# Encoder layer with expert-choice MoE on one core: norm rows in fp32r parts, gate values in one PSUM tile, last stage summed in PSUM

## The chip, the cores and the metric

The kernel runs on one core of one Trainium2 chip. The metric is the time of one execution on the device in microseconds (us). The kernel before took 981.74 us (median of three executions, 981.29 to 982.71). All times within the profile come from one more execution, which was profiled. TensorE is called PE, VectorE DVE, ScalarE ACT, GpSimd POOL and SyncE SP, as in the profile. L1208 is line 1208 of the kernel before.

## The reference

One layer over 512 tokens of width 1024, all in float32:

```python
z = x @ w_in                      # NA q|k|v, GQA q|k|v, memory q, 3 branch gates
merged = sum_g sigmoid(gate_g) * (branch_g @ w_branch_g)   # three attention mixers
x = LN(alpha * x + merged @ w_out, ln1_g, ln1_b)
aff = softmax(x @ w_router)       # 16 experts
gate, idx = top_k(aff.T, 64)      # each expert chooses 64 of 512 tokens
h = x[idx] @ w_gate_up            # 1024 -> 2 x 1024, per expert
ye = (silu(hg) * hu) @ w_down * gate
x = LN(alpha * x + scatter_add(ye), ln2_g, ln2_b)
```

The weights of the 16 experts are 192 MB, and each is read once.

## The kernel before, in words

**Stages.** The mixers run from 0 to about 452 us, w_out with the first LayerNorm, router and selection to about 523, the 16 experts from 526 to 947, and a tail of 31 us with the last quarter of the last down product, the second LayerNorm and the stores.

**Number form.** Where float32 precision is needed with the faster fp32r products, a tile is split into a high part (ACT rounds to fp32r, `hi_lo`, L85) and a low part (DVE subtracts, L86); products then run as high x high, high x low and low x high. Products with both operands in plain fp32 take PE several passes.

**Mixers.** PE works through units of weights, each split by ACT and DVE ahead of use. Attention units (`GqaUnit` and others) are interleaved with the projections of `run`, which calls small background pieces from the list `bg`; `after[i]` holds what SP is to load after weight unit i.

**Weight ring.** The experts' weights come in 192 loads of 1 MB, all issued by SP, into a ring of 22 slots of SBUF. `ring.done(...)` marks a slot as used once PE is through with it, and only then is the next load for it issued. An expert has 32 gate/up products (`gate_up`, L1208, 64 tokens stationary and 512 weight columns moving; four for each of the eight loads of 128 rows) and 32 of the down product (`down`, L1241).

**Gather.** `gather(qd)` runs before experts 0, 4, 8 and 12. It takes the tokens of four experts through one-hot matrices, and takes the gate values with eight products of 128 x 6 (L1188): two sets of four, each in a PSUM tile of tag Y, which has one buffer (tags mm, S, T and Y have 3, 2, 2 and 1). DVE adds each set up with four reductions (L1193).

**Norm rows.** The four rows ln1_g, ln1_b, ln2_g, ln2_b arrive as 32 pieces of 128 (`lnr`). `ln_row` (L1277) broadcasts a half row to all partitions with four plain fp32 products of a column of the identity with `lnr`. In expert 12 `rows_of_norm` writes the row of ln2_g on all partitions, and builds `gb`, six rows with high and low parts of ln2_g and ln2_b, by eight small products, seven DVE and two ACT operations.

**Last expert and tail** (`last_down`, L1345 on). The output columns are treated in quarters of 256. For each quarter `product(q)` makes the last expert's down product (L1366: 32 products with 64 rows, in two halves of 128 columns that lie on different partitions), `split(q)` splits it (L1375 on ACT, L1377 on DVE), and the combination with the gate matrix g adds it to the accumulator `acc`. For quarters 0 and 1 the combination goes to PSUM, DVE adds it to `acc` (L1390) and takes the statistics (L1392), and POOL multiplies by ln2_g (`times_g`, L1381). For quarters 2 and 3 the accumulator was put into PSUM ahead of time by a plain fp32 identity product in expert 15 (`preload`, L1342), PE adds onto it (L1398), DVE takes statistics out of PSUM (L1402) and multiplies by ln2_g (L1405). The products alternate between banks of tags S and T. Then 22 dummy products (`keep_warm`, L1413) follow on PE, DVE gathers mean and variance (L1434), works out 1/std (y) and −mean·y, and writes them into `ch`, PE transposes `ch` to rows (`rowT`, L1447), ACT copies the rows out (L1449), and the result is y·(acc·g) plus a low-rank product of the rows with `gb` (L1461). Five of the eight tiles of 128 x 512 are finished by DVE (L1473) and stored through SP (L1474); three by PE with a diagonal matrix (L1465) and by ACT (L1478), stored through ACT's queue (L1479).

```python
        product(3)
        add_in_psum(2)
        for m in range(NT):
            stats(2, m)
        split(3)
        add_in_psum(3)
        for mp in range(2):
            times_g_psum(2, mp)
        keep_warm(22)
```

Each engine works through its own instructions in the order in which the code issues them; an instruction waits for the last writer or reader of its tiles.

Of the kernel before, what the change touches and what calls it, by code (L numbers as in the profile page):

```python
# [9 lines left out]
F32 = mybir.dt.float32  # L10
# [4 lines left out]
ALU = mybir.AluOpType  # L15
# [26 lines left out]
def layer_kernel(ctx: ExitStack, tc: tile.TileContext, xt, xn, first0, wu, bgate, rpb, gains, wrt,  # L42
# [200 lines left out]
    lnr = cp.tile([32, P], F32, name="lnr")  # L243
    gb = cp.tile([6, D], F32R, name="gb")
    nc.sync.dma_start(lnr, lnp.rearrange("a (j n) -> (a j) n", n=P))
# [560 lines left out]


# [8 lines left out]
    at.add([GqaUnit(hp, m) for hp in range(4) for m in range(NT)])  # L816
    run(g_branch(2, True), 1.0, 3)
# [347 lines left out]
    def gather(qd):  # L1165
# [18 lines left out]
        GW[qd] = gw = small([P, 4], "gw", bufs=2)  # L1184
        for i in range(0, 4, 2):
            gp = PB("Y", f"gw{qd}{i}")
            for m in range(NT):
                nc.tensor.matmul(gp[:, 0:6], oh[:, m, i * CAP:(i + 2) * CAP],  # L1188
                                 aff3[:, m, 4 * qd + i:4 * qd + i + 2].rearrange("p e a -> p (e a)"),
                                 start=(m == 0), stop=(m == NT - 1))  # L1190
            for j in range(2):
# [30 lines left out]
    def h_transpose(e, tp=None):  # L1222
# [4 lines left out]
        t = R("G0b", [P, 4, P], f"hT{e}") if e == NEXP - 1 else R("tmp", [P, 4, P], f"hT{e}", bufs=2)  # L1227
# [45 lines left out]
    def ln_row(row, h, nm):  # L1273
        bc = PB("mm", nm)
        for j in range(4):
            r = 8 * row + 4 * h + j
            nc.tensor.matmul(bc[:, j * P:(j + 1) * P], ident[:32, r:r + 1].to_broadcast([32, P]), lnr, start=True, stop=True)  # L1277
# [37 lines left out]
    def rows_of_norm(g2):  # L1315
# [4 lines left out]
        sl, cc = (small([6, 1], n, bufs=1) for n in ("gb_s", "gb_c"))  # L1320
        nc.vector.tensor_tensor(sl, ident[:6, 4:5], ident[:6, 5:6], op=ALU.add)
        nc.vector.tensor_scalar(cc, sl, -2.0, 1.0, op0=ALU.mult, op1=ALU.add)
        sel = small([32, 8, 6], "gb_sel", bufs=1)
        for i in range(2):
            nc.vector.tensor_copy(sel[:, :, i:6:2], ident[:32, 16 + 8 * i:24 + 8 * i, None].to_broadcast([32, 8, 3]))
        for h in range(2):
            c = slice(h * 512, h * 512 + 512)
            raw = PB("mm", f"gbr{h}")
            for j in range(4):
                nc.tensor.matmul(raw[:6, j * P:(j + 1) * P], sel[:, 4 * h + j], lnr, start=True, stop=True)  # L1330
            u = R("t", [P, 512], f"gbu{h}", bufs=2)
            nc.scalar.copy(gb[:, c], raw[:6])
# [341 lines left out]
```

## Time and profile before

| | |
|---|---|
| median of three executions | 981.74 us (981.29 to 982.71) |
| the profiled execution | 980.04 us |
| its span, first to last instruction | 978.2 us |
| mean granted PE clock | 0.998 |
| busy: PE, DVE, ACT, POOL | 955.7, 451.8, 269.3, 78.0 us |
| read from HBM, written | 247.84 MB, 2.10 MB |

How to read the rows that follow: a row of the timeline gives start, duration, engine, line, operation, output and inputs by name, shapes and the number of instructions put together (x4), and in square brackets how long the engine was idle before and what ended that. A row of the windows gives busy time and count per engine (PE, PEld, DVE, ACT, POOL), then the granted PE clock, the busy share of the DMA engines and GB/s. The chain of waits is followed back from the last instruction; a row is start, duration and what was under way. In the page's slices each number stands for 24.5 us.

### The profile page before, as it was taken

How to read it: one execution, taken by the hardware profiler on the slowest of the kernel's cores; microseconds unless marked ns; L12 is line 12 of the kernel's file. 1: busy time of each engine (PE TensorE's matmuls, PEld its weight loads, DVE VectorE, ACT ScalarE, POOL GpSimd, SP SyncE). 2: the span in 40 equal slices, each digit the busy share in tenths (PEclk: the TensorE clock that was granted, in tenths of full speed). 3: DMA queues.
4: the chain of work that ended last, by engine and by line, in shares of the span. 5: the costliest groups of instructions: out<-in, count | busy, mean ns of one | idle time of the engine just before them, and what ended most of it. 6: DMA issues, size and time to landing. Idle time of an engine off the chain costs nothing.

```text
span 978.2 us, 13447 instructions
## 1 busy us (share of the span) xinstructions
PE 955.7 (98%) x5448; PEld 625.1 (64%) x5448; DVE 451.8 (46%) x852; ACT 269.3 (28%) x531; POOL 78.0 (8%) x82
## 2 busy tenths in 40 slices
PE   8999999999999999999999999999999999999997
PEld 8898887889888888887886334433343333532355
DVE  6347677664376566346463155331332223231326
ACT  6434345444354454233232010100010100100011
POOL 0102403000032231000012000000000000000002
PEclk9999999999999999999999999999999999999999
DMA  9321211211333322575829999999999999999992
GB/s 357 110 67 64 65 65 44 66 47 63 93 109 106 98 81 87 215 286 200 327 86 391 388 423 426 426 426 426 426 426 426 426 426 427 425 427 425 427 397 87
DMA packets 52318, 251.61 MB, mean 257 GB/s; under 512 B 14080, under 2 KB 14496, under 8 KB 28704
## 3 DMA queue, kind: packets, MB, share of 16 engines
q1 hardware_dynamic: 51680, 249.44, 64.5%
q10 hardware_dynamic: 576, 1.31, 0.3%
q8 instruction: 43, 0.70, 0.3%
q14 instruction: 19, 0.16, 0.0%
HBM read 247.84 MB, written 2.10 MB: 256 GB/s over the span
## 4 chain that ended last, share of the span: by engine, by line
PE 75%; DMA 12%; DVE 7%; ACT 2%; POOL 2%; issue 1%; SPq 0%; DVEq 0%; POOLq 0%; ACTq 0%
PE g L1208 9%; PE u L1208 8%; DMA gu<-in_wgu 8%; PE y L1241 8%; PE gate L253 4%; DMA dn<-in_wdn 4%; PE gate L254 4%; PE gate L255 4%; PE nqk L253 1%; PE nqk L255 1%; PE nqk L254 1%; PE gy L608 1%; PE pr L253 1%; PE ga L1173 1%; PE pr L254 1%
## 5 line engine op out<-in xcount | busy, mean ns | idle before, releaser
L1208 PE MATMUL g<-gu,xs 128*64 128x512 f32 x512 | 134.6, 604 | 1.0 <-DMA gu<-in_wgu 1.0
L1208 PE MATMUL u<-gu,xs 128*64 128x512 f32 x512 | 131.6, 592 | 0.0
L1241 PE MATMUL y<-dn,hT 128*64 128x512 f32 x480 | 106.4, 593 | 2.2 <-DMA dn<-in_wdn 2.1
L85 ACT CAST y<-y 64x512 fp32r<-64x512 f32 x30 | 17.4, 580 | 240.7 <-PE y L1241 210.8
L86 DVE TENSOR_TENSOR y<-y,y 64x512 fp32r<-64x512 f32 x30 | 20.7, 688 | 136.3 <-ACT y L85 136.3
L1208 PEld LDWEIGHTS u<-gu,xs 128*64 128x64 f32 x512 | 36.8, 137 | 73.1 <-issue 71.7
L1241 PEld LDWEIGHTS y<-dn,hT 128*64 128x64 f32 x480 | 34.0, 137 | 71.3 <-issue 63.8
L86 DVE TENSOR_TENSOR lo_twin<-raw_twin,whi 128x1024 fp32r<-128x1024 f32 x43 | 54.0, 1256 | 51.7 <-ACT whi L85 51.5
L85 ACT CAST whi<-raw_twin 128x1024 fp32r<-128x1024 f32 x64 | 67.3, 1051 | 17.6 <-PE wo L1019 8.7
L1208 PEld LDWEIGHTS g<-gu,xs 128*64 128x64 f32 x512 | 31.4, 136 | 55.5 <-issue 47.9
L1312 DVE TENSOR_TENSOR acc<-acc,cb 128x512 f32<-128x512 f32 x56 | 35.4, 682 | 35.1 <-PE cb L1310 35.1
L86 DVE TENSOR_TENSOR wlo<-raw_twin,whi 128x1024 fp32r<-128x1024 f32 x21 | 27.4, 1306 | 36.9 <-ACT whi L85 36.8
L1381 POOL TENSOR_TENSOR acc<-acc,ln2g 128x512 f32<-128x512 f32 x4 | 5.1, 1283 | 433.9 <-DVE l2s L1392 433.7
L253 PE MATMUL gate<-xha,whi 128*128 128x512 f32 x96 | 38.9, 405 | 0.0
L254 PE MATMUL gate<-xla,whi 128*128 128x512 f32 x96 | 37.5, 390 | 0.0
L253 PE MATMUL gate<-xhb,whi 128*128 128x512 f32 x96 | 37.3, 389 | 0.0
L254 PE MATMUL gate<-xlb,whi 128*128 128x512 f32 x96 | 37.3, 389 | 0.0
L584 ACT ACTIVATE P_twin<-gs,nm 128x512 f32<-128x512 f32 x32 | 21.7, 684 | 52.3 <-DVE nm L583 52.3
L1229 DVE COPY hT<-ht 128x512 f32<-128x512 f32 x15 | 10.4, 690 | 53.6 <-PE ht L1226 53.6
L1218 ACT ACTIVATE tg<-g 128x512 f32<-128x512 f32 x16 | 9.6, 597 | 89.1 <-PE g L1208 89.0
L255 PE MATMUL gate<-xha,lo_twin 128*128 128x512 f32 x80 | 31.2, 390 | 0.0
L255 PE MATMUL gate<-xhb,lo_twin 128*128 128x512 f32 x80 | 31.1, 389 | 0.0
(439 smaller groups left out, 1963.3 us busy)
## 6 DMA issues: line engine op xcount, KB each, us to landing
gu<-in_wgu SPq DMA_DIRECT2D x123, 1024.0 KB
dn<-in_wdn SPq DMA_DIRECT2D x59, 1024.0 KB
raw_twin<-in_wu SPq DMA_DIRECT2D x65, 512.0 KB
gu<-in_wgu SPq DMA_DIRECT2D x10, 512.0 KB
dn<-in_wdn SPq DMA_DIRECT2D x10, 512.0 KB
raw<-in_wu SPq DMA_DIRECT2D x8, 512.0 KB
xr<-in_xt SPq DMA_DIRECT2D x4, 512.0 KB
x<-in_xn SPq DMA_DIRECT2D x2, 1024.0 KB
```

The costliest lines, as they stand in the source:

```text
L85: nc.scalar.copy(hi, src)
L86: nc.vector.tensor_tensor(lo, src, hi.bitcast(F32), op=ALU.subtract)
L253: nc.tensor.matmul(acc, w_h, rh[:, k], start=(k == 0), stop=False)
L254: nc.tensor.matmul(acc, w_h, rl[:, k], start=False, stop=False)
L255: nc.tensor.matmul(acc, w_l, rh[:, k], start=False, stop=(k == nk - 1))
L584: nc.scalar.activation(self.p[:, h], self.s[h], AF.Exp, bias=nm[:, h:h + 1], accum_out=self.sm[:, h:h + 1])
L608: nc.tensor.matmul(self.y[h * 64:h * 64 + 64, :P], ST["vg"][:, kc, kvh * 64:kvh * 64 + 64], self.pt[:, h, kc], start=(kc == 0), stop=(kc = ...
L1173: nc.tensor.matmul(g, XH[:, m, c], oh[:, m], start=(m == 0), stop=False)
L1208: nc.tensor.matmul(GU[e][b][hf * 64:hf * 64 + 64], xs, w[b][:, hf * 512:hf * 512 + 512], start=(k == 0), stop=(k == KD - 1))
L1229: nc.vector.tensor_copy(t, tp)
L1241: nc.tensor.matmul(y[o * 64:o * 64 + 64], hT[:, c, hf * 64:hf * 64 + 64], w[j][:, o * 512:(o + 1) * 512], start=(k == 0 and j == 0), stop= ...
L1312: nc.vector.tensor_tensor(a, a, cb, op=ALU.add)
```

## The change

Four things are different.

The norm rows come as 15 rows (`_norm_rows` on the host repeats them), loaded after weight unit 14 and split in the mixers by three background pieces into `gb`, 15 x 1024 in fp32r, in which some rows hold the high and some the low part (the column `gb_s` chooses). `gsel` holds the three selecting columns; seven small DVE operations at the start build these columns. `ln_row` is one fp32r product of 15 rows and 512 columns. The preparation in expert 12 is gone.

The eight products of a gather's gate values go into one PSUM tile, all eight ahead of the reductions.

In expert 15 the accumulators of quarters 1 to 3 are split into fp32r parts (six copies on ACT, six subtractions on DVE); the preloads are fp32r products, quarter 1 in expert 15, quarter 2 behind product(0), quarter 3 between the additions of quarters 2 and 3.

In the tail, all four quarters of the last product lie in one bank, and each is split half by half. DVE adds only quarter 0 to the accumulator. Quarters 1 and 2 are summed in PSUM, copied out by ACT and multiplied by POOL; quarter 3 is multiplied by DVE. The 22 dummy products and the diagonal products are gone; four plain fp32 products (`put`) take the left halves of the accumulator to PSUM unscaled. `ch` has 13 columns with parts of −mean and of the standard deviation besides, two of them written by POOL, so that the rows can be added before ACT scales the sum by y. ACT finishes the four left halves, DVE the four right ones.

```diff
@@ -240,9 +240,15 @@
...
-    lnr = cp.tile([32, P], F32, name="lnr")
-    gb = cp.tile([6, D], F32R, name="gb")
-    nc.sync.dma_start(lnr, lnp.rearrange("a (j n) -> (a j) n", n=P))
+    gb = cp.tile([15, D], F32R, name="gb")
+    gb_s, gb_c, gb_t = (cp.tile([15, n], F32, name="gb_" + k)[:, :1] for k, n in (("s", 1), ("c", 1), ("t", 33)))
+    gsel = cp.tile([15, 3], F32R, name="gsel")
+    nc.vector.tensor_reduce(gb_s, ident[:15, 9:15], axis=AX.X, op=ALU.add)
+    nc.vector.tensor_scalar(gb_c, gb_s, -2.0, 1.0, op0=ALU.mult, op1=ALU.add)
+    for i, (a, b) in enumerate(((7, 13), (8, 14), (0, 9))):
+        nc.vector.tensor_tensor(gsel[:, i:i + 1], ident[:15, a:a + 1], ident[:15, b:b + 1], op=ALU.add)
+    nc.vector.tensor_tensor(gb_t, ident[:15, 3:4], ident[:15, 11:12], op=ALU.add)
+    nc.vector.tensor_tensor(gsel[:, 2:3], gsel[:, 2:3].bitcast(F32), gb_t, op=ALU.add)
...
@@ -804,6 +810,24 @@
...
+    norm_raw = []
...
+    def load_norms():
+        norm_raw.append(R("E0", [15, D], "norm_raw"))
+        nc.sync.dma_start(norm_raw[0], lnp)
...
+    after[14] = [load_norms]
...
+    def norm_hi():
+        nc.scalar.copy(gb, norm_raw[0])
...
+    def norm_mask():
+        norm_raw.append(R("VS", [15, D], "norm_hi"))
+        nc.vector.tensor_scalar(norm_raw[1], gb.bitcast(F32), gb_c, None, op0=ALU.mult)
...
+    def norm_lo():
+        nc.vector.scalar_tensor_tensor(gb, norm_raw[0], gb_s, norm_raw[1], op0=ALU.mult, op1=ALU.add)
...
@@ -814,6 +838,7 @@
...
     at.add([GqaUnit(hp, m) for hp in range(4) for m in range(NT)])
+    bg.extend([norm_hi, norm_mask, norm_lo])
...
@@ -1182,12 +1207,15 @@
...
+        gp2 = PB("Y", f"gw{qd}").rearrange("p (i c) -> p i c", i=2)
         for i in range(0, 4, 2):
-            gp = PB("Y", f"gw{qd}{i}")
+            gp = gp2[:, i // 2]
             for m in range(NT):
...
+        for i in range(0, 4, 2):
+            gp = gp2[:, i // 2]
...
@@ -1224,7 +1252,7 @@
...
-        t = R("G0b", [P, 4, P], f"hT{e}") if e == NEXP - 1 else R("tmp", [P, 4, P], f"hT{e}", bufs=2)
+        t = R("A0", [P, 4, P], f"hT{e}") if e == NEXP - 1 else R("tmp", [P, 4, P], f"hT{e}", bufs=2)
...
@@ -1272,9 +1300,7 @@
...
     def ln_row(row, h, nm):
...
-            r = 8 * row + 4 * h + j
-            nc.tensor.matmul(bc[:, j * P:(j + 1) * P], ident[:32, r:r + 1].to_broadcast([32, P]), lnr, start=True, stop=True)
+        nc.tensor.matmul(bc, gsel[:, row:row + 1].to_broadcast([15, P]), gb[:, h * 512:h * 512 + 512], start=True, stop=True)
...
     def residual():
@@ -1317,29 +1343,23 @@
...
-            raw = PB("mm", f"gbr{h}")
...
+    ACCP = {}
...
+    def split_acc(q, tag):
+        ACCP[q] = t = R(tag, [P, 2, NT, 256], f"accp{q}", F32R)
+        for mp in range(2):
+            m2 = slice(2 * mp, 2 * mp + 2)
+            hi_lo(t[:, 0, m2], t[:, 1, m2], ACC[mp][:, :, quarters[q]])
...
     def preload(q, banks):
...
+        t = ACCP.pop(q)
+        r = [PB(b, f"xq{q}{mp}", (P, 2, 256)) if isinstance(b, str) else b for mp, b in enumerate(banks)]
...
-            nc.tensor.matmul(r[mp], ident, ACC[mp][:, :, quarters[q]], start=True, stop=False)
+            for n in range(2):
+                nc.tensor.matmul(r[mp], ident_r, t[:, n, 2 * mp:2 * mp + 2], start=(n == 0), stop=False)
...
     def last_down(g2, xq, spare):
@@ -1352,11 +1372,11 @@
...
-        yy = [PB(b, f"yq{b}") for b in "ST"]
...
+        r = slice(64, 128)
+        yq = PB("S", "yq")
...
         def part(q, o):
...
+            return yq[64 * o:64 * o + 64, q * P:(q + 1) * P]
...
         def product(q):
...
@@ -1368,131 +1388,117 @@
...
         def split(q):
...
+                c = slice(b + o * P, b + (o + 1) * P)
+                hi_lo(yh[r, c], yl[r, c], part(q, o))
...
+        def add(q):
+            order = [(n, m) for m in range(NT) for n in range(2)] if q == 0 else [(n, m) for n in range(2) for m in range(NT)]
+            for n, m in order:
+                nc.tensor.matmul(xq[q][m // 2][:, m % 2], g[:, m], (yh, yl)[n][:, cols[q]], start=(q == 0 and n == 0),
+                                 stop=(n == 1 and (q == 0 or m % 2 == 1)))
...
+        def stats(q, m):
+            nc.vector.bn_stats(st[:, m, q], xq[q][m // 2][:, m % 2])
...
         def times_g(mp, q):
...
+        def scaled(q):
...
+                nc.scalar.copy(ACC[mp][:, :, cols[q]], xq[q][mp])
...
+        def scaled_last(q):
+            for mp in range(2):
+                nc.vector.tensor_tensor(ACC[mp][:, :, cols[q]], xq[q][mp],
+                                        g2[:, None, cols[q]].to_broadcast([P, 2, 256]), op=ALU.mult)
...
+        tl = {}
...
+        def put(m, bank):
+            tl[m, 0] = PB(bank, f"fin{m}")
+            nc.tensor.matmul(tl[m, 0], ident, acc_of(m)[:, 0:512], start=True, stop=False)
...
         product(0)
         split(0)
+        xq[2] = preload(2, (spare.rearrange("p (a b) -> p a b", a=2), "Y"))
         product(1)
         split(1)
         add(0)
+        for mp in range(2):
+            x = ACC[mp][:, :, cols[0]]
+            nc.vector.tensor_tensor(x, x, xq[0][mp], op=ALU.add)
+            for m in (2 * mp, 2 * mp + 1):
+                nc.vector.bn_stats(st[:, m, 0], acc_of(m)[:, cols[0]])
+            times_g(mp, 0)
         product(2)
         split(2)
         add(1)
+        for m in range(NT):
+            stats(1, m)
+        scaled(1)
         product(3)
-        add_in_psum(2)
+        add(2)
+        xq[3] = preload(3, ("T", "S"))
+        split(3)
         for m in range(NT):
...
-        add_in_psum(3)
...
-            times_g_psum(2, mp)
-        keep_warm(22)
+        add(3)
+        scaled(2)
+        put(0, "mm")
+        put(1, "mm")
+        put(2, "S")
+        put(3, "T")
         for m in range(NT):
...
+        mean, var = mv[:, :, 0], mv[:, :, 1]
+        nc.scalar.activation(sg, var, AF.Sqrt, bias=eps)
+        nc.vector.tensor_scalar(hv, var, LN_EPS, -0.5, op0=ALU.add, op1=ALU.mult)
+        nc.vector.tensor_scalar(ch[:, :, 3:12:8], mean[:, :, None].to_broadcast([P, NT, 2]), -1.0, None, op0=ALU.mult)
+        nc.vector.scalar_tensor_tensor(ch[:, :, 5], mean, -1.0, ch[:, :, 3].bitcast(F32), op0=ALU.mult, op1=ALU.subtract)
...
+        nc.vector.scalar_tensor_tensor(sg, hv, -2.0, y, op0=ALU.mult, op1=ALU.mult)
+        nc.gpsimd.tensor_copy(ch[:, :, 4:13:8], sg[:, :, None].to_broadcast([P, NT, 2]))
+        nc.gpsimd.tensor_tensor(ch[:, :, 6], sg, ch[:, :, 4].bitcast(F32), op=ALU.subtract)
+        nc.vector.scalar_tensor_tensor(nm, mean, -1.0, y, op0=ALU.mult, op1=ALU.mult)
+        nc.vector.tensor_copy(ch[:, :, 0:10:9], nm[:, :, None].to_broadcast([P, NT, 2]))
...
-        dg = R("tmp", [P, NT, P], "dgr", bufs=2)
...
+        rows = R("t", [P, 512], "rows", F32R, bufs=2)
+        tl[0, 1] = PB("mm", "lr0")
         for m in range(NT):
...
-        def store(m, h):
...
-            (nc.sync if h else nc.scalar).dma_start(out[:, m, c], acc_of(m)[:, c])
...
+            nc.tensor.transpose(tp[:13, m], ch[:, m].bitcast(F32), ident)
+        for a0, b0 in ((0, 1), (1, 4)):
+            nc.scalar.copy(rows[:13, a0 * P:b0 * P], tp[:13, a0:b0].rearrange("p a b -> p (a b)"))
+        for _ in range(2):
+            nc.tensor.matmul(tl[0, 1][:, :P], ident, ident, start=True, stop=True)
+        scaled_last(3)
...
+        def low_rank(m, h):
+            nc.tensor.matmul(tl[m, h], rows[:13, m * P:(m + 1) * P], gb[:13, h * 512:h * 512 + 512], start=bool(h), stop=True)
...
+        def finish(m, h):
...
+            if h:
+                nc.vector.scalar_tensor_tensor(x, x, y[:, m:m + 1], tl[m, h], op0=ALU.mult, op1=ALU.add)
+            else:
+                nc.scalar.activation(x, tl[m, h], AF.Copy, scale=y[:, m:m + 1])
+            (nc.scalar if h == 0 and m > 1 else nc.sync).dma_start(out[:, m, h * 512:h * 512 + 512], x)
...
+        for m in range(NT):
+            low_rank(m, 0)
+            if m:
+                tl[m, 1] = PB("TSY"[m - 1], f"lr{m}")
+            low_rank(m, 1)
+            finish(m, 0)
+            finish(m, 1)
...
@@ -1511,6 +1517,8 @@
...
             if e == 12:
...
+                ident_r = R("G0b", [P, P], "ident_r", F32R)
+                nc.scalar.copy(ident_r, ident)
...
@@ -1534,13 +1542,15 @@
...
-            x2 = preload(2, "ST")
...
+            split_acc(1, "E0")
+            split_acc(2, "A2")
+            gate_up(e, range(4))
+            x0 = [PB(b, f"xq0{mp}", (P, 2, 256)) for mp, b in enumerate("ST")]
...
+            split_acc(3, "A3")
...
-            x3 = preload(3, ("mm", "mm"))
+            x1q = preload(1, ("mm", "mm"))
...
@@ -1548,13 +1558,13 @@
...
+    ch = small([P, NT, 13], "ch", F32R, bufs=1)
+    nc.vector.memset(ch[:, :, 1:11:9].bitcast(F32), 1.0)
+    nc.vector.memset(ch[:, :, 7:9].bitcast(F32), 0.0)
...
+    last_down(g2, {0: x0, 1: x1q}, spare)
...
@@ -1567,6 +1577,24 @@
...
+def _norm_rows(g1, b1, g2, b2):
+    import numpy as np
+    r = np.zeros((15, 1024), np.float32)
+    for i in (0, 2, 9):
+        r[i, 512:] = g2[512:]
+    for i in (1, 10):
+        r[i, 512:] = b2[512:]
+    for i in (3, 5, 11):
+        r[i, :512] = g2[:512]
+    for i in (4, 6, 12):
+        r[i, :512] = b2[:512]
+    for i in (7, 13):
+        r[i] = g1
+    for i in (8, 14):
+        r[i] = b1
+    return r
...
 def _prep(inp):
@@ -1641,7 +1669,7 @@
...
+        "lnp": _norm_rows(*(np.asarray(inp[n])[0] for n in ("ln1_g", "ln1_b", "ln2_g", "ln2_b"))),
...
```

## What the change will do: the prediction

> **What bounds the kernel now.** I read the page first (share of the engines, bytes per slice), then the chain of waits for the stage in which a wait ends last, then windows and the timeline around each place that the change touches.
>
> ```profile
> span 978.2 us, 13447 instructions
> PE 955.7 (98%) x5448; PEld 625.1 (64%) x5448; DVE 451.8 (46%) x852; ACT 269.3 (28%) x531; POOL 78.0 (8%) x82
> GB/s 357 110 67 64 65 65 44 66 47 63 93 109 106 98 81 87 215 286 200 327 86 391 388 423 426 426 426 426 426 426 426 426 426 427 425 427 425 427 397 87
> ```
>
> PE is busy 98% of the span, but the slices of 24.5 us show that this share covers two limits: below 330 GB/s up to slice 20, where the mixers keep PE full, and a flat 426 GB/s from about 562 us to the end of the experts. There a busy PE is only paced by weights. The chain of waits says the same:
>
> ```profile
> 833.82 19.96 DMA gu<-in_wgu
> ...
> 927.42 19.58 DMA dn<-in_wdn
> ...
> 947.13 1.97 PE yqS L1366 x32
> 949.10 1.76 PE yqT L1366 x32
> ```
>
> From 833.82 to 947.00 (927.42 + 19.58) the chain holds transfers alone. The 4-us windows show where that begins:
>
> ```profile
> 548.00:552.00 4.00, 4.00 (x20) 1.15 (x16) 0.32 (x1) 0.00 (x0) 0.00 (x0) 1.00 1.01 363
> ...
> 556.00:560.00 4.00, 4.00 (x22) 1.33 (x20) 0.00 (x0) 0.00 (x0) 0.00 (x0) 1.00 1.01 428
> ```
>
> Up to about 552 us the 22-slot ring is full, a load waits until PE has used a slot, and the stream runs at 363 (last column); from 556 on it is at its ceiling of 428. So there are three regimes. Time that PE gains or loses before 552 us moves the stream and the end. Time won on PE, DVE or ACT between 552 and 947 brings nothing. From 947 on a chain over PE, ACT and DVE sets the end.
>
> **The change, part by part.** *Expert gather 0.* The two products for the gate values used one-buffer tag Y twice, so the second waited for the reductions of the first:
>
> ```profile
> 542.09 0.25 PE L1188 MATMUL gw<-aff,oh 128*128 128x6 f16 x4
> ...
> 542.38 0.67 DVE L1193 TENSOR_REDUCE gw<-gw 64x1 f32<-64x3 f32 x4 [0.40 <-PE gw L1188]
> ...
> 543.11 0.25 PE L1188 MATMUL gw<-aff,oh 128*128 128x6 f16 x4 [0.77 <-DVE gw L1193]
> 543.29 0.65 PE L1208 MATMUL g<-gu,xs 128*64 128x512 f32 x2
> ```
>
> In one tile all eight products follow one another: the second set starts about 542.27 and the 0.77 us of waiting (0.84 between the two starts that it separates) go. This lies in the slot-limited regime, so the expert work and its slot releases come earlier. Part of that is lost where the stream is already near its ceiling; bounds 0 and −0.84, taken **−0.6**. The later gathers lie after 552: 0.
>
> *Start.* Seven DVE operations on 15x1 columns now stand between the last firstl and the first low part of the weights.
>
> ```profile
> 8.37 0.96 DVE L86 TENSOR_TENSOR firstl<-first,firsth 128x768 fp32r<-128x768 f32 x1 [0.26 <-ACT firsth L85]
> ...
> 9.82 1.23 DVE L86 TENSOR_TENSOR lo_twin<-raw_twin,whi 128x1024 fp32r<-128x1024 f32 x1 [0.49 <-ACT whi L85]
> ...
> 11.10 0.39 PE L255 MATMUL mk<-firsth,lo_twin 128*128 128x256 f32 x1 [0.74 <-DVE lo_twin L86]
> ```
>
> DVE is idle 0.49 us there; PE already waits 0.74 us for that low part, and behind it is continuously busy. The 4- and 8-column operations of the tail (965.42 and 965.63 below) start 0.21 apart, as a bound 7 x 0.20 = 1.40, less 0.49: +0.9. If the short ones overlap at half of that, 0.7 − 0.49: +0.2. Taken **+0.3** (0 to +0.9), carried through the PE-bound mixers.
>
> *Hidden parts, 0.* The rows' load is on SP behind weight unit 14, where SP waits for buffers. Their three preparations fall into the attention units, where ACT and DVE have gaps:
>
> ```profile
> 173.80 0.69 ACT L584 ACTIVATE P_twin<-gs,nm 128x512 f32<-128x512 f32 x1 [2.66 <-DVE nm L583]
> ```
>
> ```profile
> 184.60 1.29 DVE L583 TENSOR_REDUCE nm<-gs 128x1 f32<-128x512 f32 x2 [1.65 <-PE gs L575]
> ```
>
> A 15x1024 operation, by the 1.2 us of a 128x1024 one (9.82 above), fits into 2.66 and 1.65. Without that cover it would be 3 x 1.2 = 3.6 us on DVE and ACT, but PE would have to lose its own lead first; bound +0.5. The broadcasts shrink from four fp32 products each to one:
>
> ```profile
> 572.13 1.15 PE L1277 MATMUL r1g<-lnr,ident 32*128 32x128 f32 x8
> ```
>
> ```profile
> 929.95 0.69 DVE L1229 COPY hT<-ht 128x512 f32<-128x512 f32 x1 [7.47 <-PE ht L1226]
> ```
>
> The first lies at 572 us, the old gb preparation in expert 12, both under the stream: 0. Expert 15 gets six high copies and six subtractions to split the accumulator (6 x 0.69 = 4.1 on DVE), inside the 7.47 idle before 929.95: 0. None of them adds a weight load.
>
> *Tail.* The rows of the timeline that carry it:
>
> ```profile
> 948.25 0.58 ACT L85 CAST y<-y 64x512 fp32r<-64x512 f32 x1 [0.75 <-DVE y L86]
> ...
> 948.87 0.69 DVE L86 TENSOR_TENSOR y<-y,y 64x512 fp32r<-64x512 f32 x1 [0.65 <-ACT y L85]
> ...
> 949.13 0.53 ACT L1375 CAST y<-yqS 64x128 fp32r<-64x128 f32 x2 [0.30 <-PE yqS L1366]
> 949.70 0.59 DVE L1377 TENSOR_TENSOR y<-yqS,y 64x128 fp32r<-64x128 f32 x2
> ...
> 952.07 0.69 DVE L1390 TENSOR_TENSOR acc<-acc,spare 128x512 f32<-128x512 f32 x1
> 952.79 0.75 DVE L1392 BATCH_NORM_STATS2 l2s<-acc 128x6 f32<-128x256 f32 x2
> ...
> 953.68 2.66 POOL L1381 TENSOR_TENSOR acc<-acc,ln2g 128x512 f32<-128x512 f32 x2 [432.95 <-DVE l2s L1392]
> ...
> 961.33 6.33 PE L1413 MATMUL spare<-ident 128*128 128x128 f32 x44
> 961.60 0.42 DVE L1402 BATCH_NORM_STATS2 l2s<-xq 128x6 f32<-128x256 f32 x1
> ...
> 965.42 0.17 DVE L1442 CAST ch<-l2m 128x8 fp32r<-128x8 f32 x1
> 965.63 0.17 DVE L1443 TENSOR_TENSOR ch<-l2m,ch 128x4 fp32r<-128x4 f32 x1
> ...
> 967.50 0.60 PE L1447 MATMUL rowT<-ident,ch 128*6 128x128 f32 x4
> ...
> 968.14 0.57 ACT L1449 CAST rows<-rowT 6x512 fp32r<-6x512 f32 x1 [3.75 <-PE rowT L1447]
> ...
> 969.38 3.50 DVE L1473 SCALAR_TENSOR_TENSOR acc<-acc,l2y,lr 128x512 f32<-128x512 f32 x5 [2.39 <-PE lr L1461]
> 970.15 3.09 SPq L1474 DMA_DIRECT2D out<-acc  x5
> ...
> 975.33 0.34 ACTq L1479 DMA_DIRECT2D out<-acc  x1
> ```
>
> Added wait: the four quarters of the last product now share one bank, and in the program's order product(q) waits until both halves of split(q−1) are done. Halves go in turn over ACT and DVE, which the pair at 948.25 and 948.87 shows with 0.04 us handovers: 0.27 + 0.30 + 0.27 + 0.30 plus handovers, about 1.3. So product(1) starts at 950.5 instead of 948.9; behind it on PE stand the preloads and adds. Split 1 ends at 953.75, and DVE begins quarter 0 there instead of 952.07: 2 x 0.69 + 2 x 0.75 = 2.9, to 956.6. Half of split 2 is behind that on DVE, so product(3) starts about 957.6 (2.6 later than before).
>
> Removed from DVE: the additions of quarter 1 (2 x 0.69; PE now adds it onto a preloaded accumulator, as it did for quarters 2 and 3) and the two multiplications of quarter 2 (1.3; POOL does them): 2.7 in all. Product 3 ends at 959.55, split 3 at 960.8, the preload of quarter 3 at 961.4, its additions at 962.35. Statistics of quarter 3 begin there instead of 961.60: +0.75. The small operations behind, 961.60 to 965.80 (965.63 + 0.17) before, gain two that do not fit beside the square root (0.1) and two on POOL (0.2): ready at 966.85.
>
> Before, the columns were ready at 965.80 and rowT ran at 967.50, because the 44 warming pieces held PE until 967.66 (961.33 + 6.33). They are gone; four fp32 products of the accumulator, 512 columns each, stand there instead: by r1g above (512 columns in fp32, 1.0 to the next start) 4.0, from 962.4 to 966.4. So rowT runs at about 966.9: −0.6. From rowT to the first store was 970.15 − 967.50 = 2.65: copy, product, 0.70 on DVE. Now the copy's first part is 128 columns, and ACT finishes the first tile with some 0.58 (948.25, 512 columns too): about 2.2, −0.45. First store at 969.1.
>
> ```profile
> 957.00:960.50 3.50, 1.70 (x13) 1.50 (x13) 3.41 (x11) 0.52 (x2) 2.56 (x2) 1.00 0.00 0
> 960.50:964.00 3.50, 3.50 (x17) 3.50 (x18) 3.36 (x10) 0.00 (x0) 0.00 (x0) 0.51 0.00 0
> ...
> 971.00:975.00 4.00, 3.64 (x9) 1.15 (x8) 1.84 (x3) 1.46 (x3) 0.00 (x0) 1.00 1.04 400
> 975.00:977.00 2.00, 0.00 (x0) 0.00 (x0) 0.00 (x0) 0.30 (x1) 0.00 (x0) 1.00 0.65 249
> ```
>
> The 2.1 MB of output move at 400 GB/s; 5.24 us if nothing interrupts them, against 5.65 from 971.0 to some 976.65, since the last issue was at 975.33. With ACT and DVE each finishing four tiles, the last issue is about 971.5 and the queue never runs dry: −0.4. Tail: −0.6 − 0.45 − 0.4 = **−1.45**, bounds 0 and −2.2.
>
> **Sum.** −0.6 + 0.3 − 1.45 = −1.75. The profiled execution took 980.04 (span 978.2), which becomes 978.29; it lies 1.70 below the median of 981.74, so against that the time is 980.0.
>
> **Rivals.** *No gain: the one-bank wait takes all that the additions gave.* Speaking for it: DVE is rid of 2.7 us, yet quarter 3 comes 0.75 later, and the splits are in series with the products, so 0.35 more for each of four is +1.4, the whole gain. Against it: the 0.04 handovers. Without the tail's gain: 981.4.
>
> *More gain.* Start free, the gather's whole 0.84, tail −2.0: 978.9.
>
> *Slower: POOL.* It gets six multiplications instead of four and both last columns ahead of rowT stand behind them. From 955.2, at 1.33 (953.68 above), the fifth waits for the copies of quarter 2 (962.8) and the sixth ends near 965.4, 1.2 before its columns are due. From about 1.9 us each it decides; at 2.5 it is 955.2 + 15.0 + 0.2 = 970.4 instead of 966.85: +3.55, 983.5. Against it: the rows at 1.33 were taken beside a busy DVE.
>
> *The clock.* In the rows 957.00 and 960.50 a stretch with PE busy 1.70 of 3.50 is followed by 3.5 us at 0.51. The change gives PE the preload and additions there and no idle time over 1 us, so I expect 1.00. If the gate still falls once, over additions and the four products, rowT comes 0.9 later: 980.9; if twice, 984. The Trainium skill ("TensorE: Matmul & The Clock Gate", Part 1) says that after one idle window of some 3.4 us the array goes to half speed; the trace agrees in the length, but its window was half busy, so the gate is harsher here than the page says. By the page alone nothing throttles and the forecast stands.
>
> **How the numbers follow.** Forecast (979.1 to 980.9) 0.42; more gain (978.2 to 979.1) 0.16; no gain, the clock falling once among it (980.9 to 983.0), 0.28; slower by POOL 0.08, by the clock twice 0.06. The range takes the first three with their bounds: 978.4 to 983.0. A measurement tells about 0.2% (1.96 us) from no change: below 979.78 are a little over half of the forecast (0.24) and the gain (0.16), so faster 0.40; slower 0.14; same 0.46.
>
> **What would show it.** Products of the gate values without a wait; first low part at 10.1 rather than 9.82; product(1) of the last expert 3.4 us behind product(0) rather than 1.8; clock 1.00 to the end; rowT 19.8 behind product(0) rather than 20.4; POOL's multiplications at 1.3; first store 22.0 behind product(0) rather than 23.0 and a store rate of 400 without a dip. It is wrong if the transfers' stretch before 947 moves by over 1 us, or if POOL or PE holds rowT.

## The result, and the profile of the changed kernel

The changed kernel takes 978.63 us (median of 8 executions, 977.14 to 980.60) against 981.75 (8 executions, 979.28 to 982.71) on the same chips: ratio 0.997, with a 95% interval of 0.9957 to 0.9982, or 2.9 us less (1.8 to 4.2). A second series on another chip gave 0.9969 (0.9958 to 0.9981). The profiled execution took 977.14 with a span of 975.3, so the spans differ by 2.9 too. The forecast was 980.0, a gain of 1.75: right in sign, and too small. The time lies in the band that the prediction had given to its rival of more gain (978.2 to 979.1, chance 0.16), below the band of the forecast itself (979.1 to 980.9, chance 0.42).

The page of the changed kernel, its span and its first part:

```profile
span 975.3 us, 13272 instructions
## 1 busy us (share of the span) xinstructions
PE 945.4 (97%) x5350; PEld 612.6 (63%) x5350; DVE 452.3 (46%) x857; ACT 274.5 (28%) x540; POOL 80.2 (8%) x86
```

PE is 10 us less busy (955.7 before), DVE as busy as before, and the span is shorter by only 2.9. Of what PE was spared, 5.0 lay between 526 and 946, beside the stream of weights, and 5.3 behind 946, where the dummy products are gone. Where the 2.9 are from shows in two places. The first gather, timeline of the changed kernel:

```profile
542.19 0.35 PE L1214 MATMUL gw<-aff,oh 128*128 128x6 f16 x8
542.47 1.08 PE L1236 MATMUL g<-gu,xs 128*64 128x512 f32 x4
```

Expert 0 goes on 0.28 behind the first of the eight products, 1.20 before (542.09 to 543.29). The last stage starts at 946.08 instead of 947.13. The tail, timeline of the changed kernel:

```profile
946.08 1.97 PE L1386 MATMUL yq<-dn,hT 128*64 128x128 f32 x32 [0.61 <-DMA dn<-in_wdn]
...
949.34 1.97 PE L1386 MATMUL yq<-dn,hT 128*64 128x128 f32 x32 [0.16 <-DVE y L86]
...
956.43 1.97 PE L1386 MATMUL yq<-dn,hT 128*64 128x128 f32 x32 [0.71 <-DVE y L86]
...
961.25 3.60 PE L1423 MATMUL fin<-acc,ident 128*128 128x512 f32 x8
...
961.28 2.50 POOL L1407 TENSOR_TENSOR acc<-acc,ln2g 128x512 f32<-128x512 f32 x2 [0.82 <-ACT acc L1411]
...
965.39 0.22 POOL L1469 TENSOR_TENSOR ch<-l2v,ch 128x4 fp32r<-128x4 f32 x1
...
965.69 0.60 PE L1477 MATMUL rowT<-ident,ch 128*13 128x128 f32 x4 [0.84 <-POOL ch L1469]
...
966.32 0.62 ACT L1479 CAST rows<-rowT 13x128 fp32r<-13x128 f32 x2 [2.30 <-PE rowT L1477]
...
967.95 3.46 SPq L1493 DMA_DIRECT2D out<-acc  x6
...
970.23 0.34 ACTq L1493 DMA_DIRECT2D out<-acc  x1
```

The new wait is there (0.16 <-DVE, then 0.71 <-DVE), and product(1) starts 3.26 behind product(0) instead of 1.77. Yet rowT comes 19.61 behind product(0) instead of 20.37, because nothing but its columns holds it (<-POOL ch), and the first store is 2.26 behind rowT instead of 2.65. The windows of the changed kernel over the stores (last column GB/s, third from the end the PE clock):

```profile
968.00:969.00 1.00, 1.00 (x4) 0.42 (x2) 1.00 (x3) 1.00 (x2) 0.00 (x0) 0.58 0.19 76
969.00:970.00 1.00, 0.19 (x1) 0.00 (x0) 1.00 (x2) 0.57 (x2) 0.00 (x0) 0.50 1.04 399
973.00:974.00 1.00, 0.00 (x0) 0.00 (x0) 0.00 (x0) 0.00 (x0) 0.00 (x0) 0.50 1.04 399
974.00:975.30 1.30, 0.00 (x0) 0.00 (x0) 0.00 (x0) 0.00 (x0) 0.00 (x0) 0.50 0.02 5
```

The stores run without a dip from 968.8 to 974.1. The clock was 1.00 up to 968 and falls to 0.50 behind that, where the forecast had 1.00 to the end; the stores' rate doesn't show it. Counted from product(0), the tail is 975.3 − 946.08 = 29.22 against 31.07, 1.85 less: 0.76 up to rowT, 0.39 from there to the first store, and 0.64 in the data (6.18 from the first store to the last packet at 974.13; before, 6.82 to 976.97). The 0.06 that is left lies behind the last packet. With the 1.05 ahead of it that is 2.9.

### The profile page after: what moved, and what is told of

Read it like the earlier page. It is cut to its first block, busy times and chain, and to the rows that moved or that the text cites. A ratio compares the mean times of both kernels' runs of the same rounds, so it can differ in the third digit from the quotient of the medians.

```text
span 975.3 us, 13272 instructions
## 1 busy us (share of the span) xinstructions
PE 945.4 (97%) x5350; PEld 612.6 (63%) x5350; DVE 452.3 (46%) x857; ACT 274.5 (28%) x540; POOL 80.2 (8%) x86
## 3 DMA queue, kind: packets, MB, share of 16 engines
q10 hardware_dynamic: 432, 1.05, 0.3%
## 4 chain that ended last, share of the span: by engine, by line
PE 71%; DMA 16%; DVE 7%; ACT 2%; POOL 2%; issue 1%; SPq 0%; DVEq 0%; POOLq 0%; ACTq 0%
DMA gu<-in_wgu 9%; PE g L1236 8%; PE u L1236 7%; PE y L1269 6%; DMA dn<-in_wdn 6%; PE gate L259 4%; PE gate L261 4%; PE gate L260 4%; PE ga L1198 2%; PE nqk L261 1%; PE nqk L260 1%; PE nqk L259 1%; PE gy L614 1%; PE pr L259 1%; PE ga L1200 1%
## 5 line engine op out<-in xcount | busy, mean ns | idle before, releaser
L1407 POOL TENSOR_TENSOR acc<-acc,ln2g 128x512 f32<-128x512 f32 x6 | 7.6, 1280 | 435.4 <-DVE l2s L1435 433.4
L261 PE MATMUL gate<-xhb,lo_twin 128*128 128x512 f32 x80 | 31.1, 389 | 0.0
```

The source lines that it names most:

```text
L261: nc.tensor.matmul(acc, w_l, rh[:, k], start=False, stop=(k == nk - 1))
```

## The experiments

The theory after the result was that of the prediction with larger terms: the gather's wait counts in full since it lies where the ring of slots holds the stream, the tail gives the rest, and the other edits are hidden. The rivals were that the stream absorbs the gather's gain, that the cheaper broadcasts give it, and that the one-bank wait or POOL's queue is on the tail's path. Ratios are to the kernel before on the same chips. Single terms are read from the traces.

One interval needs care. The profiled executions reach the first gather at times 2.4 us apart, since some have a half-clock stretch earlier, as here in the run of the gather alone (the kernel before had 1.00 in both windows):

```profile
520.00:524.00 4.00, 3.31 (x45) 3.04 (x46) 2.04 (x9) 0.49 (x2) 1.68 (x2) 0.81 1.04 416
524.00:528.00 4.00, 4.00 (x27) 2.92 (x27) 1.29 (x4) 0.56 (x1) 0.00 (x0) 0.76 1.01 416
```

So the part up to the tail is compared from the first gate-value product to product(0) of the last stage, called the stretch below, and the tail from product(0). In the kernel before the stretch is 947.13 − 542.09 = 405.04, in the changed one 946.08 − 542.19 = 403.89.

**The gather alone, undone alone, and in the later gathers.** The edit in the kernel before (in the second run the old form in the changed kernel for `qd == 0` alone, in the third for `qd > 0` alone):

```diff
+        gp2 = PB("Y", f"gw{qd}").rearrange("p (i c) -> p i c", i=2)
-            gp = PB("Y", f"gw{qd}{i}")
+            gp = gp2[:, i // 2]
...
+        for i in range(0, 4, 2):
+            gp = gp2[:, i // 2]
```

> The kernel before with only the gate values in one PSUM tile; nothing else is changed. Theory (PE time before about 552 us moves the whole stream of weights): the second set of products no longer waits 0.77 us, expert 0 resumes 0.8 to 0.9 earlier, the last load lands 0.8 to 1.0 earlier, the tail behind it takes as long as in the kernel before (31.1 from the first product of the last quarter stage to the end); time 0.9 below before. Rival (the stream's ceiling absorbs it): the last load lands within 0.3 of before, and the time is the same.

> The changed kernel with the old two tiles in the first gather alone. Theory: the wait of 0.77 is back, the last load lands 0.8 to 1.0 later than in the changed kernel, time 2.1 below before instead of 3.1. Rival (absorbed): no later landing, time 3.1 below before.

> The changed kernel with the old two tiles in the second, third and fourth gather. Theory (from 556 us on the stream is at its ceiling): three waits of 0.8 are back on PE and the last load lands within 0.2 of the changed kernel; time 3.1 below before. Rival (every wait of PE counts): 2.4 later, time 0.7 below before.

Measured: alone 0.9985 (0.9969 to 1.0001), 1.5 less, an interval that just reaches no change, with a stretch of 404.39. The tail up to rowT is that of the kernel before (20.40). Behind rowT it isn't, against the expectation: in this execution the clock falls to 0.50 at 973, where it held 1.00 in the kernel before, the last diagonal products take 2.07 instead of 1.13, the last store goes out 30.3 behind product(0) instead of 28.2, and the tail is 33.2 long instead of 31.1. So the old tail can differ by 2 us between two executions. Timeline of this run:

```profile
974.96 2.07 PE L1468 MATMUL lr<-acc,dgr 128*128 128x512 f32 x2
...
978.45 0.34 ACTq L1482 DMA_DIRECT2D out<-acc  x1
```

Undone in the first gather: 0.9975 (0.9960 to 0.9989), 2.5 less, stretch 406.47. Undone in the later three: 0.9967 (0.9955 to 0.9979), 3.2 less, stretch 403.93. Over all profiles the new form in the first gather (nine, without the two that repeat the broadcasts near 580) has 403.9 to 404.5, the old form 405.0, 405.2 and 406.5. The means differ by 0.9 without the 406.5, as long as the wait that went, but not all of that is the stream of weights. Adding up the DMA packets of a trace gives the time, counted from the first gate-value product, at which 100 of the 249.6 MB that come ahead of the output are still missing. It is 175.7 in the kernel before and in the run below without dummy products, 175.4 with the gather's edit alone, and 175.0 to 175.3 in the other eight with the new form. The rest of the difference comes at the end of the stretch, where product(0) starts while 2.2 to 2.5 MB are still to come in the nine (2.5 in the changed kernel, 2.3 in the kernel before), which is scatter. So the wait of the first gather of 0.9 costs some 0.4 to 0.5 of stream, not the whole that the theory said, and those of the later ones cost nothing; the times alone, with intervals of 1.2 us each way, would not have shown it. The 406.47 lies 1.3 above the other two with the old form. Its stream was already about 1 us behind the others at the gather itself, before the wait could act, and its window of 552 to 556 still ran at 363 GB/s; why is open.

**The dummy products of the kernel before.** The edit is one line:

```diff
-        keep_warm(22)
```

> The kernel before without the 22 dummy products ahead of the statistics of the last quarter. Theory (they held rowT for 1.6): rowT runs at once behind its columns, 18.8 instead of 20.4 behind the first product of the last stage, time 1.5 below before. Rival (they keep the clock up, and without them it falls): the clock is near 0.5 from rowT on, the products behind take twice as long (about 6 us of them on the path), and the time is the same or up to 2 above before.

Measured: 1.0035 (1.0022 to 1.0047), 3.4 more. The theory had rowT right and the time wrong; the rival had the clock and the doubled products right, and its bound of 2 on the loss too low. Windows and timeline of this run:

```profile
960.50:964.00 3.50, 1.20 (x4) 0.91 (x4) 3.35 (x11) 0.00 (x0) 0.00 (x0) 0.57 0.00 0
964.00:968.00 4.00, 1.51 (x8) 1.28 (x9) 3.11 (x13) 0.76 (x2) 0.00 (x0) 0.50 0.00 0
968.00:972.00 4.00, 4.00 (x9) 1.81 (x8) 2.06 (x3) 1.00 (x4) 0.00 (x0) 0.50 0.19 72
```

```profile
966.49 1.01 PE L1446 MATMUL rowT<-ident,ch 128*6 128x128 f32 x4 [4.34 <-DVE ch L1442]
...
970.29 2.08 PE L1464 MATMUL lr<-acc,dgr 128*128 128x512 f32 x2
970.40 4.92 SPq L1473 DMA_DIRECT2D out<-acc  x5
...
980.09 0.34 ACTq L1478 DMA_DIRECT2D out<-acc  x1
```

rowT does come 1.55 earlier (18.82 behind product(0)), held by its columns alone. But the clock stays at 0.50 to the end, the diagonal products take 2.08 instead of 1.12, and the last store goes out 32.4 behind product(0) instead of 28.2. The changed kernel gets the early rowT without that price: its four identity products (3.60 at 961.25), work that the end needs, stand on PE there, and its clock is 1.00 up to 968. That it is these products that keep the clock was not tested by a run without them; the idle time of 1.8 on PE ahead of 960.41 is gone in the changed kernel too.

**The dummy products put back.**

```diff
         put(3, "T")
+        tl[0, 1] = PB("mm", "lr0")
+        for _ in range(22):
+            nc.tensor.matmul(tl[0, 1][:, :P], ident, ident, start=True, stop=True)
```

> The changed kernel with the 22 dummy products put back behind the four identity products and ahead of rowT. Theory (what stands on PE ahead of rowT holds it): 44 pieces at 0.06 to 0.13 end 2.7 to 5.7 after the identity products (18.8 behind product 0), so rowT comes at 21.5 to 24 instead of 19.6 and the time is 0 to 1 above before. Rival (rowT waits for its columns anyway): no change, 3.1 below before.

```profile
965.27 5.07 PE L1457 MATMUL lr<-ident 128*128 128x128 f32 x44
970.18 0.60 PE L1479 MATMUL rowT<-ident,ch 128*13 128x128 f32 x4
```

Measured: rowT 23.52 behind product(0), 1.0014 (1.0004 to 1.0024), 1.4 above the kernel before, a little more than the theory's 0 to 1, and over 4 above the changed one. The 44 pieces took 5.07. What stands on PE ahead of rowT holds it.

**Two banks.**

```diff
-        yq = PB("S", "yq")
+        yy = [PB(t, "yq" + t) for t in "ST"]
...
-            return yq[64 * o:64 * o + 64, q * P:(q + 1) * P]
+            return yy[q % 2][64 * o:64 * o + 64, q // 2 * P:(q // 2 + 1) * P]
```

> The changed kernel with the quarters of the last product alternating between two PSUM banks, as before the change; all else as changed. Theory (the one-bank wait is on the path): product 1 follows product 0 at once behind the preload (2.9 instead of 3.26), product 3 starts about 1.8 earlier, rowT 17.8 instead of 19.6 behind product 0, time 1.5 to 1.9 below the changed kernel (4.6 to 5.0 below before). Rival (DVE's additions and statistics bound the stage, the wait lies beside them): rowT within 0.4 of the changed kernel, time 3.1 to 3.5 below before.

Measured: 0.997 (0.9958 to 0.9981), as the changed kernel; rowT 19.25, 0.36 earlier. The theory falls in its time. Product(3) does start 1.24 earlier (9.11 behind product(0) instead of 10.35), but the gain is lost behind it. Timeline:

```profile
956.28 1.97 PE L1386 MATMUL yqT<-dn,hT 128*64 128x128 f32 x32
...
958.11 1.25 ACT L1411 COPY acc<-xq 128x512 f32<-128x512 f32 x2 [1.21 <-DVE l2s L1403]
...
959.38 0.26 ACT L85 CAST y<-yqT 64x128 fp32r<-64x128 f32 x1
```

The product ends at 958.25, and its split waits until 959.38 behind ACT's copies of quarter 1. The rival had the sizes right and named DVE; what took the gain was ACT's queue.

**Two more multiplications on POOL.**

```diff
         scaled(2)
+        scr = R("A2", [P, 2, 256], "scr")
+        nc.gpsimd.memset(scr, 1.0)
+        for _ in range(2):
+            nc.gpsimd.tensor_tensor(scr, scr, g2[:, None, cols[2]].to_broadcast([P, 2, 256]), op=ALU.mult)
```

> The changed kernel with two more multiplications of 128x512 on POOL (on a scratch tile, not used) ahead of its two column operations. POOL ended its sixth multiplication 1.34 before its columns were due. Theory (POOL is beside the path with 1.3 of slack): the two take 2.6 and a fill of some 0.3 stands with them, so rowT comes 1.5 later, time 1.6 below before. Rival (POOL's queue is already on the path): rowT 2.8 later, time 0.3 below before.

Measured: rowT 21.71, 2.10 later, and 1.0012 (0.9999 to 1.0024), 1.2 above the kernel before. rowT lies between the two expectations, the time above both, and the way was one that neither named. Timeline:

```profile
965.97 2.63 POOL L1454 TENSOR_TENSOR scr<-scr,ln2g 128x512 f32<-128x512 f32 x2
...
966.25 1.03 DVE L1468 TENSOR_TENSOR l2a<-l2y 128x4 f32<-128x4 f32 x1
967.31 0.16 DVE L1469 TENSOR_TENSOR l2a<-l2a,l2h 128x4 f32<-128x4 f32 x1
967.51 1.11 DVE L1470 SCALAR_TENSOR_TENSOR l2y<-l2a,l2y 128x4 f32<-128x4 f32 x1
...
969.46 1.01 PE L1481 MATMUL rowT<-ident,ch 128*13 128x128 f32 x4 [2.95 <-POOL ch L1473]
```

Two DVE operations on 4 columns, 0.16 each in the changed kernel, take 1.03 and 1.11: each begins inside a POOL multiplication and ends with it. So it is DVE's chain that was held, not POOL's own two operations. Then PE was idle for 2.95, its clock fell to 0.50 at about 969, and rowT took 1.01 instead of 0.60; the first store came 3.38 behind rowT instead of 2.26. The Trainium skill ("SBUF — State Buffer", section "Who interferes with whom") says that a DVE instruction with two SBUF inputs contends with a GpSimd instruction that reads SBUF, and calls the port pair that they share an exclusive lock; the trace agrees, at 1.03 and 1.11 against 0.16. The one between them, at 967.31, fell between the two multiplications and took its 0.16.

**The broadcasts eight times over, then the same PE time with full rows, then in expert 12 alone.**

```diff
+        for _ in range(8):
             nc.tensor.matmul(bc, gsel[:, row:row + 1].to_broadcast([15, P]), gb[:, h * 512:h * 512 + 512], start=True, stop=True)
```

> The changed kernel with each broadcast of a norm row made eight times over (the result is the same). PE does 6 x 7 x about 0.25 = 10 us more, all after 556 us, beside the stream. Theory (hidden): the last load lands within 0.2, time 3.1 below before. Rival (the cheaper broadcasts are where the gain is from): 5 to 10 later.

```diff
+        for _ in range(8):
+            nc.tensor.matmul(bc[:, :P], ident, ident, start=True, stop=True)
         nc.tensor.matmul(bc, gsel[:, row:row + 1].to_broadcast([15, P]), gb[:, h * 512:h * 512 + 512], start=True, stop=True)
```

> The changed kernel with eight products of the full identity (128 rows, plain fp32, 128 columns) ahead of each of the six broadcasts; what they write is overwritten. They take PE about as long (1.8 each, 10.6 in all) as the seven repeated 15-row products of the run before, after which the granted clock fell to 0.5 three times and the last quarter stage began 8.2 later against expert 0. Theory (the gate takes 15 rows of 128 for idleness): no dip of the clock at 576, 592 and 848, and the last stage begins only 3 to 5 later, the rest of the 7 of the first four broadcasts having been hidden. Rival (PE has no lead over the stream at 572 to 592, so its time counts in full): 7 to 8 later without any dip.

```diff
+        for _ in range(8 if row == 2 else 1):
             nc.tensor.matmul(bc, gsel[:, row:row + 1].to_broadcast([15, P]), gb[:, h * 512:h * 512 + 512], start=True, stop=True)
```

> The changed kernel with only the two broadcasts of ln2_g, in expert 12, made eight times over, 3.5 on PE near 848. Theory (the lead of PE over the stream has grown by then): the last stage begins within 0.3 of the changed kernel against expert 0, time 2.5 to 3.1 below before, even if the clock dips there. Rival (PE's time counts at any place): 3.5 to 5 later, time 0.4 to 2 above before.

Measured: the first 1.004 (1.0025 to 1.0054), 3.9 above the kernel before, stretch 412.53, 8.3 above the usual 404.2. The theory that all was hidden falls, and there were two reasons: the clock, and the time on PE itself. The run with full rows separates them: 1.0015 (1.0006 to 1.0025), stretch 408.94, 4.7 above. Windows of the first, then of the second run, whose last two rows stand behind its second gather (626 to 633):

```profile
592.00:596.00 4.00, 4.00 (x14) 2.39 (x15) 2.96 (x3) 0.00 (x0) 0.00 (x0) 0.74 1.02 428
596.00:600.00 4.00, 4.00 (x12) 1.18 (x10) 1.75 (x2) 0.00 (x0) 0.00 (x0) 0.50 0.94 377
```

```profile
592.00:596.00 4.00, 4.00 (x25) 2.56 (x27) 3.95 (x4) 0.00 (x0) 0.00 (x0) 1.00 1.02 430
596.00:600.00 4.00, 4.00 (x22) 1.37 (x20) 1.27 (x2) 0.60 (x1) 0.00 (x0) 1.00 1.01 401
...
636.00:640.00 4.00, 4.00 (x22) 1.48 (x20) 0.51 (x1) 0.00 (x0) 0.00 (x0) 1.00 0.95 297
640.00:644.00 4.00, 4.00 (x22) 1.30 (x19) 0.18 (x1) 0.00 (x0) 0.00 (x0) 1.00 0.90 320
```

In the first run PE had only 15-row products from 590.80 to 595.28. The clock falls to 0.50 although PE is busy throughout; with 128 rows it stays at 1.00. The two kinds of product differ in number form and columns too, but the experts' own products, with 128 rows and 512 columns at the same pace (four in 1.08 at 542.47 above), run at 1.00 throughout, which leaves the rows as the likeliest difference; the values in the tiles were not varied. Some 3.6 of the 8.3 or more are due to that, since the first run adds no more PE time than the second. The other 4.7 come without any dip. They are what is left of 7.9 us that were added to the four broadcasts (4 x 1.98, the timeline of the second run), so about 3 us of them were hidden by PE's lead over the stream. By the packets of the trace only 2.1 of the 4.7 were lost by 606; the rest was lost at the second gather, behind which the stream ran at 297 and 320 GB/s, where the changed kernel has 426 to 428 behind its own. So the lead that the broadcasts use up is missing at the next gather.

```profile
589.49 2.05 PE L1304 MATMUL r1g<-ident 128*128 128x128 f32 x16
591.47 0.49 PE L1305 MATMUL r1g<-gb,gsel 15*128 15x512 f32 x1
```

In expert 12 alone the repetition cost nothing: 0.9966 (0.9952 to 0.9979), stretch 404.18, in spite of a clock of 0.58 in the window from 844. So hidden holds for expert 12, and near 580 only up to some 3 us beyond the single broadcasts (0.49 at 571.31).

**A reordered version.** Two banks as above, and:

```diff
-        scaled(1)
         product(3)
...
         split(3)
+        scaled(1)
...
-                times_g(mp, q)
+                if q == 1:
+                    times_g(mp, q)
...
         nc.gpsimd.tensor_tensor(ch[:, :, 6], sg, ch[:, :, 4].bitcast(F32), op=ALU.subtract)
+        for mp in range(2):
+            times_g(mp, 2)
```

> The changed kernel with two banks for the quarters as in the run of two banks, ACT's copies of quarter 1 moved behind the split of quarter 3, and POOL's two column operations moved ahead of its multiplications of quarter 2. Theory (behind the bank wait stood ACT's queue: the split of quarter 3 waited 1.1 for copies; and POOL's multiplications must not run beside DVE's small operations): split 3 starts as product 3 ends, rowT 18.4 to 18.9 behind product 0 instead of 19.6, first store 20.7 to 21.2, time 0.7 to 1.2 below the changed kernel. Rival (the identity products, which wait for POOL's quarter 1, or DVE's statistics hold rowT): rowT 19.2 or later, no gain.

> The changed kernel once more, on the chip of the run of the reordered one, so that the two are compared there: 2.5 to 3.5 below before, rowT 19.6 behind product 0.

```profile
957.38 1.97 PE L1386 MATMUL yqT<-dn,hT 128*64 128x128 f32 x32
...
959.40 0.26 ACT L85 CAST y<-yqT 64x128 fp32r<-64x128 f32 x1 [1.40 <-PE yqT L1386]
...
966.53 2.52 POOL L1407 TENSOR_TENSOR acc<-acc,ln2g 128x512 f32<-128x512 f32 x2
966.65 0.60 PE L1480 MATMUL rowT<-ident,ch 128*13 128x128 f32 x4 [0.52 <-POOL ch L1470]
...
968.92 3.63 SPq L1496 DMA_DIRECT2D out<-acc  x6
```

Measured: product(0) of this run stood at 948.27, so rowT comes 18.38 behind it and the first store 20.65, both 1.2 earlier than in the changed kernel (19.61 and 21.87, the same in its second series). The split of quarter 3 now starts as its product ends. The time is 0.9958 (0.9945 to 0.9971), the changed kernel on that chip 0.9969 (0.9958 to 0.9981): 1.1 less, as in the trace, though the two intervals overlap. It is the fastest version tried, 4.1 below the kernel before. The three moves were made together; of two banks alone the 0.36 above is known, and of the other two no run tells what each is worth.

## Why the prediction was right, and where its sizes were off

The regimes were right in kind: waits of PE in the first gather moved the end, waits in later gathers did not. The mechanism of each term of the sum held, with the sizes below. The time came out where the rival of more gain had it (978.9, with a free start, the gather's whole 0.84 and 2.0 in the tail), and the range held because it took that rival in. Of the rival's terms the first and the last came about; the second shows in the profiles, but only half of it in the stream.

*The gather, −0.6.* About right. The wait itself went in full (0.28 to expert 0 instead of 1.20), and part of it was lost to the stream's ceiling, as forecast: with 100 MB to come, the stream of the changed kernel is 0.5 ahead, counted from the gather (175.20 instead of 175.74), and 0.4 with the gather's edit alone. That the start of the last stage moved by 1.05 is in part luck of the two profiled executions, by the scatter of the place at which product(0) starts. The ceiling from 556 us on was not quite one either: the window of 568 to 572 ran at 395 GB/s before and at 422 in the changed kernel.

*The start, +0.3.* Measured +0.07. The seven operations are short and overlap, timeline of the changed kernel:

```profile
9.19 0.14 DVE L246 TENSOR_REDUCE gb_s<-ident 15x1 f32<-15x6 f32 x1
...
9.81 0.15 DVE L251 TENSOR_TENSOR gsel<-gsel,gb_t 15x1 fp32r<-15x1 f32 x1
9.89 1.22 DVE L86 TENSOR_TENSOR lo_twin<-raw_twin,whi 128x1024 fp32r<-128x1024 f32 x1
...
11.17 0.39 PE L261 MATMUL mk<-firsth,lo_twin 128*128 128x256 f32 x1 [0.87 <-DVE lo_twin L86]
```

All seven stand in 0.77, and they begin before the last firstl ends, so the low part comes 0.62 behind the end of firstl instead of 0.49. Those that don't wait for one another start 0.07 apart; I had used the 0.2 of chained operations.

*Hidden parts, 0.* Held in sum: the kernel with the gather's edit alone and the changed one differ by 0.5 in the stretch, as the nine profiles with that form do among themselves, and by 0.2 in the stream. My ground for the broadcasts was too broad, though. I took everything behind 556 us as hidden; the repeated broadcasts showed a lead of only some 3 us at 580.

*The tail, −1.45.* Measured −1.85. Up to rowT −0.76 for −0.6 (19.61 against 19.8 forecast), to the first store −0.39 for −0.45, the data −0.64 for −0.4. The last is the term that was mis-sized: I had put the end of the old data at 976.65, and its last packet is at 976.97. The added wait was priced right (3.26 for 3.4 forecast), and its rival, that it would eat the whole gain, fell, though not for want of a price: without the wait rowT came only 0.36 earlier, but with ACT's and POOL's queues put in order as well 1.2.

*POOL and the clock.* POOL's multiplications took 1.25 to 1.33 each, as forecast. The clock held 1.00 only up to 968 and not to the end, while PE ran the products of 13 rows, with an idle time of 0.84 just ahead of rowT; as the stores went at 399 to 408 GB/s all the same, it cost nothing that shows. The working for POOL was wrong in its mechanism: its point of decision was put at the queue ahead of POOL's own two operations, and the run with two more multiplications showed that DVE's small operations are held first. In the changed kernel POOL's sixth multiplication ends at 963.78, and the DVE operations with two SBUF inputs behind it are these:

```profile
964.01 0.17 DVE L1462 SCALAR_TENSOR_TENSOR ch<-l2mv,ch 128x4 fp32r<-128x4 f32 x1
...
964.29 0.16 DVE L1464 TENSOR_TENSOR l2a<-l2y 128x4 f32<-128x4 f32 x1
```

So the margin was 0.2 to the first and 0.5 to the one that was held, and not 1.2.

*The signs and the chances.* Of the two signs of being wrong, the first came true by a hair: the end of the transfers' stretch moved by 1.05 where 1 was the bound, half of it in the stream. The second did not: the last column that rowT waits for is POOL's, but POOL had been idle for 1.34 ahead of its two operations. In the working of the chances, the share of the forecast's band that lies below 979.78 is 0.38 (0.68 of 1.8), not a little over half, so the 0.40 for faster was some 0.08 too high by its own numbers; and the range ends at 978.4 where its lowest band ends at 978.2.

The sum of −1.75 became −2.9: −0.3 forecast ahead of the tail was −1.05 (+0.1 up to the first gather, −0.5 in the stream, and −0.6 at the start of the last stage, which had no term and is within the scatter), and −1.45 in it was −1.85. Without that scatter the traces account for some 2.3, which lies within the interval of the times (1.8 to 4.2) as 2.9 does.

## What to carry to other kernels

A ring of slots makes two kinds of time out of one kind of wait: while loads wait for released slots, an engine's wait moves the end, here by about half of its length, and behind that only the lead that has grown since can hide work, so size the lead and don't only name the regime. Before a queue is relieved, look at what stands second: here the bank wait hid ACT's copies, and only moving both, with POOL's multiplications, gained 1.2. Where PE needs work to keep its clock, work that the end needs anyway is better than dummy products, which held rowT by 3.9 when they were put back.

## What the runs showed of the hardware that was not expected

Products with 15 rows do not hold the clock: some 4 us of them, with PE busy all the time, brought the granted clock to 0.50, and with 128 rows it stayed at 1.00. The Trainium skill ("TensorE: Matmul & The Clock Gate", Part 1) speaks of how busy PE has been over a window of some 3.4 us; here the rows in use seem to count as well. A POOL multiplication holds a 4-column DVE operation with two SBUF inputs for up to 1.11 instead of 0.16. And a half-clock stretch near 100 or 520 us, present in some profiled executions and absent in others of kernels that are alike up to there, goes with a first gather that comes up to 2.4 us later, more than most of the terms here.
